# Two sums of the down weights moved to VectorE, and an embedding gate by plain products

## The chip, the cores and the metric

The kernel runs on one core of a Trainium2 chip. Its time is the device time of one execution in microseconds (us); given are the median and the extremes of several. A profile is taken of one further execution. The engines are TensorE (PE, matrix products into PSUM banks), VectorE (DVE), ScalarE (ACT), GpSimd (POOL) and SyncE (SP); the last two, and ScalarE now and then, issue DMAs.

## The reference

One layer of a decoder trunk in fp32 for 512 tokens, width 1024, feed-forward width 2816. The change touches its two last parts:

```python
for i in range(DEPTH):                     # DEPTH = 1
    ...
    h = rmsnorm(x, ffn_norm[i])
    x = x + conv_ffn(h, w_up[i], conv_w[i], conv_b[i], w_down[i])
    gate = jax.nn.sigmoid((rmsnorm(x, ple_norm[i]) @ w_ple_gate[i]).astype(jnp.float32)).astype(x.dtype)
    x = x + gate * (p[i] @ w_ple[i])
return rmsnorm(x, final_norm)
```

`conv_ffn` is a product with w_up (1024 x 5632), a causal convolution of width 3, gelu(a) * b, and a product with w_down (2816 x 1024).

## The kernel before

**Products.** Every fp32 product is three fp32r matmuls of split operands (`mm3`, L203 to L207): high by high, high by low, low by high. Weights come as raw blocks of 128x1024 and are split by `parts` (L64): a cast on ScalarE gives the high part (L69), a subtraction on VectorE the low part (L70). The parts go to four rotating buffers, or, with `spare`, to the pool of 37 blocks (`blk`) that also holds raw blocks and operands.

**Queue of weights.** `plan`, `plan_seven`, `prepare` and `take` (L89 to L160) form one list of units, in the order in which the products use them. A unit is a load (DMA) and a cut (sums and split). Four loads are issued ahead of the cut that is due, and two cuts are made ahead of the product that takes them. So loads stand on SyncE's queue, and casts and subtractions on ScalarE's and VectorE's, in program order among everything else that these engines do.

**Seven products for eight.** `seven` (L349) computes a product of 2x2 blocks with seven block products P1 to P7 of combined operands. The weights are quartered into a, b, c, d. Combined weights: P1 takes a, P5 a+b, P6 a+b+c, P7 b+c, P4 a+b+c+d, P2 d, P3 c. P6, P7 and P4 accumulate into two PSUM banks (`seeded`, sd) that start as copies of P1. Behind P6, and again behind P7, ScalarE copies these banks out (`u`, L372); the next product that adds to them waits for the copies. `minus` (L374) subtracts on VectorE, and a drain takes each finished quarter.

**Down product.** The loop over the 22 blocks of the feed-forward width makes the combined operands; after eight, sixteen and 22 blocks the down product runs for 4, 4 and 3 pairs of blocks (`PARTS`, L37) by `seven` in the order P1 P5 P2 P6 P7 P4 P3 (`DOWN`): rounds one, two and three below. Its weights are planned with `adds="all"` (L198): a block t starts as b, GpSimd DMAs that accumulate add a (for P5), then c (for P6, issued after P5's split, L141), then d (for P4, after P6's split); a block s starts as b, and a GpSimd DMA adds c (for P7). Each for two chunks (two contraction tiles each) of a round: eight accumulating DMAs a round. The drain adds the result to x (L682).

**Gate.** After round three x's columns are turned by TensorE transposes (`turn_half`, L720), scaled on ScalarE, combined on VectorE and split. Between the two halves of the tokens stands the embedding product p @ w_ple for the first two token tiles (`embed`, L648; the other two were made earlier, put into the DRAM tile `ple_d`, and are read back at L745). The gate's product is `seven` in the order P5 P1 P6 P7 P4 P2 P3 (`LAST`) with the quartered w_g planned with `adds="some"` (L201): a and c (for s) by GpSimd DMAs, c for P6 and d for P4 by sums on VectorE (L138). `tail` halves the last quarter. `drain_g` (L765) applies sigmoid, multiplies by the embedding, adds to x, squares, and for a finished token tile makes the reciprocal root on GpSimd (`rstd_1`, L608), scales by it and the final norm's weights `gB`, and writes out.

Of the kernel before, what the change touches and what calls it, by code (L numbers as in the profile page):

```python
# [7 lines left out]
F32 = mybir.dt.float32  # L8
# [26 lines left out]
DOWN = ("P1", "P5", "P2", "P6", "P7", "P4", "P3")  # L35
LAST = ("P5", "P1", "P6", "P7", "P4", "P2", "P3")
PARTS = ((0, 4), (4, 4), (8, 3))  # L37
# [8 lines left out]
def trunk(ctx, tc, xT, xr, pT, wsT, par, bsp, w_u0, w_u1, w_v, w_ga, w_gb, w_p, w_pl,  # L46
# [46 lines left out]
    def plan_seven(w, order=INNER, adds="vector", spare=(), q0=0, n=HK):  # L93
# [25 lines left out]
        def unit(prod, ch):  # L119
            inplace = adds == "vector"  # L120
            t = "a" if inplace else "t"
            need = {"P1": [("a", "a")], "P5": [("b", "b")] if inplace else [("t", "b", "a")],
                    "P6": [] if adds == "all" else [("c", "c")], "P7": [] if inplace else [("s", "b", "c")],
                    "P4": [] if adds == "all" else [("d", "d")], "P2": [("d", "d")], "P3": [("c", "c")]}[prod]
            dst = {"P1": "a", "P5": t, "P6": t, "P7": "b" if inplace else "s", "P4": t, "P2": "d", "P3": "c"}[prod]
            extra = {"P5": "b" if inplace else None, "P6": "c", "P7": "c" if inplace else None, "P4": "d"}.get(prod)
            if adds == "all":
                extra = None
            cols = ch[1] * T

# [12 lines left out]

            todo.append((load, cut))

        for prod in order:
            for ch in pairs_of(n):
                unit(prod, ch)

# [22 lines left out]
    for w in (w_v, w_ga, w_gb):  # L172
        plan_seven(blocks(w))

# [16 lines left out]
    for i in range(KF):  # L191
# [156 lines left out]

    def seven(op, drain, order=INNER, fill=(), tail=False):  # L349

        fill = list(fill)
        n = len(op)
        ahead = AHEAD + 2 if tail else AHEAD
        bank_of = {}
# [3 lines left out]
        def step(o, c, w, ch, first):  # L360
            for j, c0, m, t in o:
                for i in range(ch[1]):
                    k = ch[0] + i
                    a = op[k][c]
                    a = [a[:, z, j * P:(j + 1) * P] for z in range(2)]
                    mm3(t, a, [z[:, c0:c0 + m] for z in wslice(w, i, T)], first and k == 0, k == n - 1,
                        skip_group_check=True)

# [4 lines left out]

        def minus(p, z):  # L374
            j, c0, m, t = p
            o = z[j][:, c0:c0 + m]
            V.tensor_tensor(o, t, o, op=ALU.subtract)
            return o

        for prod in order:  # L380
            b, c = ops[prod]
            if b not in bank_of:
                bank_of[b] = [(j, 0, T, seeded[j] if b == "b" else bank()) for j in range(2 if b != "c" or not tail else 1)]
                if b == "c" and tail:
                    bank_of[b] += [(1, 0, H, bank()[:, :H]), (1, H, H, bank()[:, :H])]
            o = bank_of[b]
            first = b != "b" and b not in begun
            begun.add(b)
            if prod == "P3" and tail:
                ws = [take(ahead) for _ in pairs_of(n)]  # L390
                for p in o:
                    for w, ch in zip(ws, pairs_of(n)):
                        step([p], c, w, ch, False)
                    drain(0, p[0], 1, minus(p, u[0]), p[1])
                continue
            for ch in pairs_of(n):
                step(o, c, take(ahead), ch, first)
                if fill:
                    fill.pop(0)()
            if prod == "P1":  # L400
                for j in range(2):
                    S.copy(seeded[j], o[j][3])
            elif prod == "P6":
                copies(0)
            elif prod == "P7":
                copies(1)
                for p in bank_of["c"]:
                    minus(p, u[1])
                for j in range(2):
                    drain(1, j, 1, u[1][j], 0)  # L410
            elif prod == "P4":
                for j in range(2):
                    drain(1, j, 0, seeded[j], 0)
            elif prod == "P2":
                for p in o:
                    drain(0, p[0], 0, p[3], 0)
            elif prod == "P3":
                for p in o:
                    drain(0, p[0], 1, minus(p, u[0]), 0)
        for f in fill:  # L420
# [67 lines left out]

    def drain_v(th, j, fh, src, c0):
        b = 2 * th + j  # L490
# [33 lines left out]
    def gate(op, fill=()):  # L524
        g = [None] * NT

        def drain(th, j, fh, src, c0):
            b = 2 * th + j
# [150 lines left out]
    def drain_x(last):  # L679
        def drain(th, j, fh, src, c0):  # L680
            b = 2 * th + j
# [37 lines left out]

    def turn_half(th, k):  # L720
        tp = bank()
        for i, f in enumerate((k, HK + k)):
            for j in range(2):
                PE.transpose(tp[:, (2 * i + j) * P:(2 * i + j + 1) * P], columns(x, 2 * th + j, f), ident)
        t = block("xf", (4, H))
        for i, f in enumerate((k, HK + k)):
            S.activation(t[:, i], tp[:, i * H:(i + 1) * H], AF.Copy, scale=col(C_PLE, f))  # L727
        return t

    G1 = []  # L730
    for k in range(HK):
        t = turn_half(1, k)
        V.tensor_tensor(t[:, 2], t[:, 0], t[:, 1], op=ALU.subtract)
        z = halves(t[:, 1:3], 2)
        G1.append((t, z))
    ple = [block("ple") for _ in range(NT)]
# [10 lines left out]
    for k in range(HK):  # L747
# [5 lines left out]
        if k % 2 == 0:  # L753
            t2 = block("s2", (2, 2, H), F32R)
        cut_into(t2[:, k % 2], t1[:, 3])
        z0, z3 = halves(t[:, 0:2], 2), halves(t[:, 2:4], 2)
        XE.append(dict(A11=z0[:, 0], A12=z0[:, 1], A22=z1[:, 0], D=z1[:, 1], S2=t2[:, k % 2], S3=z3[:, 0], E=z3[:, 1]))
    r_emb = [rstd_1([xss[b][:, 0:1], xss[b][:, 1:2]]) for b in range(NT)]


    fss = [small.tile([P, 3], F32, tag="fss", name="fss", bufs=NT) for _ in range(NT)]
    seen = [0] * NT
    done = [0] * NT

    def drain_g(th, j, fh, src, c0):  # L765
        b = 2 * th + j
        n = src.shape[-1]
        last = b == 1
        pc = ple[b][:, fh, c0:c0 + n]
        xc = x[b][:, fh, c0:c0 + n]  # L770
        S.activation(src, src, AF.Sigmoid, scale=r_emb[b])
        V.tensor_tensor(pc, src, pc, op=ALU.mult)
        V.tensor_tensor(xc, xc, pc, op=ALU.add)  # L773
        S.activation(src, xc, AF.Square, accum_out=fss[b][:, seen[b]:seen[b] + 1])
        if last:
            V.tensor_tensor(pc, xc, gB[:, fh * T + c0:fh * T + c0 + n], op=ALU.mult)
        seen[b] += 1
        done[b] += n
        if done[b] == D:
            r = rstd_1([fss[b][:, i:i + 1] for i in range(seen[b])])  # L780
            for g in range(2):
                ot = ple[b][:, g]
                if not last:
                    V.scalar_tensor_tensor(ot, x[b][:, g], r, gB[:, g * T:(g + 1) * T], op0=ALU.mult, op1=ALU.mult)  # L784
                elif g:
                    S.activation(ot, ot, AF.Copy, scale=r)
                else:
                    V.tensor_scalar_mul(ot, ot, r)
                nc.sync.dma_start(out[b, :, g * T:(g + 1) * T], ot)

    seven(XE, drain_g, LAST, tail=True)


# [4 lines left out]
def _layout(i):  # L798
# [22 lines left out]
    def pairs(z):  # L821
# [25 lines left out]
        "w_dn": a["w_down"][0].reshape(KF // 2, 2, P, 2, T).transpose(1, 3, 0, 2, 4).reshape(4, KF // 2, P, T),  # L847
        "w_g": sv(a["w_ple_gate"][0]),
        "w_ple": a["w_ple"][0].reshape(2, P, D),
# [17 lines left out]
```

## Time and profile before

| | |
|---|---|
| median of 3 runs | 807.81 us (807.12 to 807.92) |
| profiled execution, its own time | 809.77 us |
| its span in the trace | 808.1 us |
| its mean granted TensorE clock | 0.986 |
| TensorE busy | 773.3 us (96%) |
| VectorE busy | 553.9 us (69%) |
| ScalarE busy | 389.6 us (48%) |
| GpSimd busy | 60.5 us (7%) |

Times in the rows are microseconds from the start of the span. Busy shares are means over stages with different limits; matmuls overlap in the pipeline, so one lasts longer (0.39 us) than the distance to the next. "idle before <-releaser" is the time for which the engine had nothing to do, and what ended it. A granted clock of 1.00 is 2.4 GHz.

### The profile page before, as it was taken

To read this page: it belongs to the slowest core of one execution; us is meant where nothing else is said; L and a number is where in the kernel's file an instruction comes from. 1 tells how busy PE (TensorE), PEld (TensorE's weight loads), DVE (VectorE), ACT (ScalarE), POOL (GpSimd) and SP (SyncE) were. 2 spreads that over 40 slices of the span, in tenths; PEclk is the share of its full clock that TensorE was granted. 3 is DMA by queue.
4 is the path that set the end of the run, shared out by engine and by line. 5 is a ranking of instruction groups with operands and counts; after the bars stand their busy time and mean duration, and the time that the engine had idled before them with its cause. 6 is when DMAs were issued, how large, how long until landed. Compare 5 with 4: busy or idle time off the path is not lost.

```text
span 808.1 us, 9316 instructions
## 1 busy us (share of the span) xinstructions
PE 773.3 (96%) x3458; PEld 635.6 (79%) x3458; DVE 553.9 (69%) x783; ACT 389.6 (48%) x566; POOL 60.5 (7%) x95
## 2 busy tenths in 40 slices
PE   9999999999999999999999997999999799999793
PEld 7888888888888887888888875888888588877673
DVE  7796988774666646336766663676774566778896
ACT  6676745562232324225644543345443434467873
POOL 0000100000122000000000021000013010031101
PEclk9999999999999999999999998999999899999997
DMA  9612225152044256006422369631229862391712
GB/s 350 253 53 79 78 79 183 53 191 96 1 156 150 85 173 218 1 1 268 174 53 66 91 133 269 216 93 46 78 79 212 244 168 78 107 194 26 239 22 104
DMA packets 42493, 104.26 MB, mean 129 GB/s; under 512 B 3664, under 2 KB 3792, under 8 KB 42448
## 3 DMA queue, kind: packets, MB, share of 16 engines
q1 hardware_dynamic: 33760, 85.73, 30.3%
q0 software_dynamic: 7104, 13.63, 10.0%
q10 hardware_dynamic: 1584, 4.31, 1.6%
q8 instruction: 27, 0.44, 0.2%
q14 instruction: 18, 0.15, 0.1%
HBM read 100.51 MB, written 3.15 MB: 128 GB/s over the span
## 4 chain that ended last, share of the span: by engine, by line
PE 47%; issue 27%; DMA 11%; DVE 8%; ACT 5%; POOL 1%; POOLq 0%; SPq 0%; ACTq 0%; DVEq 0%
PE mm L205 10%; PE mm L206 10%; PE mm L207 10%; DMA raw<-in_w_dn 9%; PE sd L205 6%; PE sd L206 6%; PE sd L207 6%; DVE wlo L70 2%; ACT whi L69 2%; DMA pt<-in_pT 1%; DVE raw L138 1%; POOL raw L106 1%; PE mm L514 1%; DVE x L773 0%; DVE ple L784 0%
## 5 line engine op out<-in xcount | busy, mean ns | idle before, releaser
L70 DVE TENSOR_TENSOR wlo<-raw,whi 128x1024 fp32r<-128x1024 f32 (+1 forms) x192 | 225.3, 1182 | 184.2 <-ACT whi L69 183.6
L69 ACT CAST whi<-raw 128x1024 fp32r<-128x1024 f32 (+1 forms) x185 | 189.8, 1032 | 232.4 <-PE mm L206 56.2
L206 PE MATMUL mm<-blk,whi 128*128 128x512 f32 x480 | 186.8, 389 | 0.0
L205 PE MATMUL mm<-blk,whi 128*128 128x512 f32 x480 | 186.4, 390 | 0.3 <-ACT blk L240 0.3
L207 PE MATMUL mm<-blk,wlo 128*128 128x512 f32 x480 | 186.6, 389 | 0.0
L205 PEld LDWEIGHTS mm<-blk,whi 128*128 128x128 f32 x480 | 90.0, 188 | 19.6 <-ACT blk L240 0.9
L206 PEld LDWEIGHTS mm<-blk,whi 128*128 128x128 f32 x480 | 90.1, 188 | 18.8
L207 PEld LDWEIGHTS mm<-blk,wlo 128*128 128x128 f32 x480 | 90.1, 188 | 18.6
L205 PE MATMUL mm<-whi,blk 128*128 128x512 f32 x214 | 83.9, 392 | 1.2 <-ACT xf L727 1.2
L206 PE MATMUL mm<-wlo,blk 128*128 128x512 f32 x214 | 83.4, 390 | 0.0
L207 PE MATMUL mm<-whi,blk 128*128 128x512 f32 x214 | 83.3, 389 | 0.0
L205 PE MATMUL sd<-whi,cmb 128*128 128x512 f32 x108 | 45.5, 421 | 12.8 <-ACT u L372 12.3
L205 PE MATMUL mm<-whi,cmb 128*128 128x512 f32 (+1 forms) x132 | 50.1, 380 | 2.1 <-ACT xf L727 1.8
L106 POOL DMA_DIRECT2D raw<-in_w_dn x24 | 27.9, 1389 | 321.9 <-DVE wlo L70 207.6
L206 PE MATMUL mm<-wlo,cmb 128*128 128x512 f32 (+1 forms) x132 | 49.8, 377 | 0.4 <-DVE wlo L70 0.4
L207 PE MATMUL mm<-whi,cmb 128*128 128x512 f32 (+1 forms) x132 | 49.3, 376 | 0.0
L205 PEld LDWEIGHTS mm<-whi,blk 128*128 128x128 f32 x214 | 40.2, 188 | 10.3 <-ACT xf L727 2.0
L207 PEld LDWEIGHTS mm<-whi,blk 128*128 128x128 f32 x214 | 40.2, 188 | 8.3
L206 PEld LDWEIGHTS mm<-wlo,blk 128*128 128x128 f32 x214 | 40.2, 188 | 8.2
L206 PE MATMUL sd<-wlo,cmb 128*128 128x512 f32 x108 | 44.3, 410 | 0.3 <-DVE wlo L70 0.3
L207 PE MATMUL sd<-whi,cmb 128*128 128x512 f32 x108 | 43.9, 408 | 0.0
L205 PE MATMUL sd<-whi,blk 128*128 128x512 f32 x110 | 43.1, 392 | 0.5 <-ACT u L372 0.5
(184 smaller groups left out, 1037.2 us busy)
## 6 DMA issues: line engine op xcount, KB each, us to landing
raw<-in_w_up SPq DMA_DIRECT2D x44, 512.0 KB, 5.5
raw<-in_w_dn SPq DMA_DIRECT2D x25, 512.0 KB, 3.4
raw<-in_w_dn POOLq DMA_DIRECT2D x20, 512.0 KB, 7.8
raw<-in_w_g SPq DMA_DIRECT2D x10, 512.0 KB, 6.7
raw<-in_w_v SPq DMA_DIRECT2D x8, 512.0 KB, 11.4
raw<-in_w_ga SPq DMA_DIRECT2D x8, 512.0 KB, 4.0
raw<-in_w_gb SPq DMA_DIRECT2D x8, 512.0 KB, 3.6
raw<-in_w_p SPq DMA_DIRECT2D x8, 512.0 KB, 4.8
```

The lines of the kernel that those rows point to most:

```text
L69: (V.tensor_copy if first else S.copy)(hi[:, :cols], raw[:, :cols])
L70: V.tensor_tensor(lo[:, :cols], raw[:, :cols], hi[:, :cols].bitcast(F32), op=ALU.subtract)
L106: (G if kw else nc.sync).dma_start(o, block_of(name, ch), **kw)
L138: V.tensor_tensor(z[:, :cols], z[:, :cols], raw[extra, ch][:, :cols], op=ALU.add)
L205: PE.matmul(o, wh, ah, start=first, stop=False, **kw)
L206: PE.matmul(o, wh, al, start=False, stop=False, **kw)
L207: PE.matmul(o, wl, ah, start=False, stop=last, **kw)
L514: PE.matmul(mx[:, n * P:(n + 1) * P], vt[n].rearrange("p a t -> p (a t)")[:, f * P:(f + 1) * P], wsm[:, f, :], start=True, stop=True)
```

## The change

**Down weights.** `plan_seven` is called with `"some"` instead of `"all"`: c (for P6) and d (for P4) are loaded to blocks of their own and added by VectorE in the unit's cut. a for P5 and c for P7 still come by accumulating GpSimd DMAs. c's block is loaded for P6 and kept for P3, so that the number of plain loads stays ten a round. VectorE gets four sums a round (rounds one and two: of 128x1024; round three: two of 128x1024 and two of 128x512), GpSimd loses four DMAs.

**Gate.** w_g is eight plain blocks (128 rows by 1024 columns), all split once into blocks that are kept. The operands are only turned and split. Token tiles run in the order 2, 3, 0, 1; each has eight contraction steps for two banks (the last tile: one bank of 512 columns, then two of 256). The second half's columns are turned ahead of token tile 3. The multiplication by gB now stands ahead of the reciprocal root for all tiles. `tail`, `LAST` and the column argument of the drains are gone.

```diff
-            plan_seven(blocks(w_dn), DOWN, "all", q0=part[0], n=part[1])
+            todo.extend(plan_seven(blocks(w_dn), DOWN, "some", q0=part[0], n=part[1]))
     for k in range(2):
         plan(w_ple[k])
-    plan_seven(blocks(w_g), LAST, "some", spare=("P3",))
+    for k in range(KD):
+        plan(w_g[k], spare=True)
...
-    def turn_half(th, k):
...
+    def turn_half(th):
+        got = []
+        for k in range(HK):
+            tp = bank()
+            t = block("xe", (2, 2, H), F32R)
+            for i, f in enumerate((k, HK + k)):
+                for j in range(2):
+                    PE.transpose(tp[:, (2 * i + j) * P:(2 * i + j + 1) * P], columns(x, 2 * th + j, f), ident)
+            for i, f in enumerate((k, HK + k)):
+                split_into(t[:, i], tp[:, i * H:(i + 1) * H], col(C_PLE, f))
+            got.append(t)
+        return got
+
+    XE = [None, turn_half(1)]
...
-    XE = []
-    for k in range(HK):
-        t1, z1 = G1[k]
-        t = turn_half(0, k)
-        V.tensor_tensor(t1[:, 3], t1[:, 2], t[:, 0], op=ALU.subtract)
-        V.tensor_tensor(t[:, 2], t[:, 0], t1[:, 0], op=ALU.subtract)
-        V.tensor_tensor(t[:, 3], t[:, 1], t1[:, 3], op=ALU.add)
...
+    wg = [take() for _ in range(KD)]
...
-    seven(XE, drain_g, LAST, tail=True)
+    for b in (2, 3, 0, 1):
+        th, j = divmod(b, 2)
         last = b == 1
...
+        if b == 3:
+            XE[0] = turn_half(0)
+
         if last:
+            groups = [[(bank(), 0)], [(bank()[:, :H], T)], [(bank()[:, :H], T + H)]]
+        else:
+            groups = [[(bank(), 0), (bank(), T)]]
+        fss = small.tile([P, 3], F32, tag="fss", name="fss")
+        n = 0
+        for group in groups:
+            for k in range(KD):
+                a = XE[th][k % HK][:, k // HK]
+                a = [a[:, z, j * P:(j + 1) * P] for z in range(2)]
+                for ob, c0 in group:
+                    mm3(ob, a, [z[:, c0:c0 + ob.shape[-1]] for z in wg[k]], k == 0, k == KD - 1)
+            for ob, c0 in group:
...
+                S.activation(ob, ob, AF.Sigmoid, scale=r_emb[b])
+                V.tensor_tensor(pc, ob, pc, op=ALU.mult)
+                V.tensor_tensor(xc, xc, pc, op=ALU.add)
+                S.activation(ob, xc, AF.Square, accum_out=fss[:, n:n + 1])
+                V.tensor_tensor(pc, xc, gB[:, c0:c0 + w], op=ALU.mult)
+                n += 1
```

Below stand the orders of single engines, of the program before and of the changed one. Line numbers are those of the program that the rows come from; they are smaller in the changed one.

GpSimd's queue in round one of the down product, before. raw_3629 and raw_3686 are the blocks t of the two chunks, raw_3819 and raw_3838 the blocks s; what stands in brackets are the semaphores of the instructions waited for (DVE: VectorE, DMAHW: plain loads, DMASW: GpSimd's own DMAs).

```order
L106 DMA raw_3629<-in_w_dn 128x2x512 [waits DMAHW5_49,DMAHW2_49,DMAHW6_49,DMAHW0_49,DVE_49]
L106 DMA raw_3629<-in_w_dn 128x2x512 [waits DMASW0_49,DVE_49]
L106 DMA raw_3686<-in_w_dn 128x2x512 [waits DMAHW5_49,DMAHW3_49,PE_49]
L106 DMA raw_3686<-in_w_dn 128x2x512 [waits DMASW2_49,DVE_49]
L106 DMA raw_3819<-in_w_dn 128x2x512 [waits DMAHW4_49,DMAHW6_49,DMAHW0_49,PE_49]
L106 DMA raw_3838<-in_w_dn 128x2x512 [waits DMAHW7_49]
L106 DMA raw_3629<-in_w_dn 128x2x512 [waits DMASW1_49,DVE_49]
L106 DMA raw_3686<-in_w_dn 128x2x512 [waits DMASW3_49,DVE_49]
```

The same queue in the changed program: round one's four (raw_3629 and raw_3686 are t, raw_3821 and raw_3840 are s), and the first of round two.

```order
L105 DMA raw_3629<-in_w_dn 128x2x512 [waits DMAHW5_49,DMAHW2_49,DMAHW6_49,DMAHW0_49,DVE_49]
L105 DMA raw_3686<-in_w_dn 128x2x512 [waits DMAHW5_49,DMAHW3_49,DVE_49]
L105 DMA raw_3821<-in_w_dn 128x2x512 [waits DMAHW5_49,DMAHW4_49,DMAHW7_49,DMAHW0_49,DVE_49]
L105 DMA raw_3840<-in_w_dn 128x2x512 [waits DMAHW5_49,DMAHW7_49,DMAHW1_49,DVE_49]
L105 DMA raw_4553<-in_w_dn 128x2x512 [waits DMAHW4_49,DMAHW0_49,DVE_49]
```

The second and third writes into t are gone, and the two DMAs into s stand directly behind the first writes. The waits for VectorE that are left are for buffers that come free, no longer for splits of this round.

VectorE in round three, before, from the splits for P6 on. raw_5241 (128x1024) and raw_5286 (128x512) are t of the two chunks; x_2521 and x_2522 are the sums that drain P2; raw_5425 and raw_5438 are s, for P7.

```order
L70 TENSOR_TENSOR wlo_5442<-raw_5241,whi_5441 128x1024
L70 TENSOR_TENSOR wlo_5459<-raw_5286,whi_5458 128x512
L682 TENSOR_TENSOR x_2521<-mm_5373,x_2521 128x512
L682 TENSOR_TENSOR x_2522<-mm_5374,x_2522 128x512
L611 TENSOR_SCALAR fms_5810<-xss_3034 128x1
L611 TENSOR_SCALAR fms_5815<-xss_3035 128x1
L70 TENSOR_TENSOR wlo_5476<-raw_5425,whi_5475 128x1024
L70 TENSOR_TENSOR wlo_5494<-raw_5438,whi_5493 128x512
```

VectorE at the same place in the changed program; raw_5393 and raw_5409 are c, raw_5318 and raw_5375 are d, raw_5427 is s.

```order
L137 TENSOR_TENSOR raw_5241<-raw_5241,raw_5393 128x1024
L137 TENSOR_TENSOR raw_5286<-raw_5286,raw_5409 128x512
L666 TENSOR_TENSOR x_2521<-mm_5373,x_2521 128x512
L69 TENSOR_TENSOR wlo_5445<-raw_5241,whi_5444 128x1024
L69 TENSOR_TENSOR wlo_5462<-raw_5286,whi_5461 128x512
L666 TENSOR_TENSOR x_2522<-mm_5374,x_2522 128x512
L137 TENSOR_TENSOR raw_5241<-raw_5241,raw_5318 128x1024
L137 TENSOR_TENSOR raw_5286<-raw_5286,raw_5375 128x512
L595 TENSOR_SCALAR fms_5722<-xss_3034 128x1
L595 TENSOR_SCALAR fms_5727<-xss_3035 128x1
L69 TENSOR_TENSOR wlo_5478<-raw_5427,whi_5477 128x1024
```

The sums for P6 stand ahead of P2's drain and the splits for P6 between its two halves; the sums for P4 come ahead of the split for P7.

SyncE's queue at the gate, before, from the embedding's weights on.

```order
L82 DMA raw<-in_w_ple 128x1024 x2
L106 DMA raw<-in_w_g 128x2x512 x5
L745 DMA ple<-ple_d 128x512 x4
L106 DMA raw<-in_w_g 128x2x512 x5
L789 DMA out<-ple 128x512 x8
```

The same queue in the changed program.

```order
L81 DMA raw<-in_w_ple 128x1024 x2
L81 DMA raw<-in_w_g 128x1024 x6
L727 DMA ple<-ple_d 128x512 x4
L81 DMA raw<-in_w_g 128x1024 x2
L768 DMA out<-ple 128x512 x8
```

Six blocks of w_g instead of five quarters' chunks stand ahead of the reads of ple_d, two instead of five behind them.

## Rows read from the trace of the kernel before

**Rows 1.** The page: busy time with share of span; granted clock in 40 slices.

```profile
PE 773.3 (96%) x3458; PEld 635.6 (79%) x3458; DVE 553.9 (69%) x783; ACT 389.6 (48%) x566; POOL 60.5 (7%) x95
...
PEclk9999999999999999999999998999999899999997
```

**Rows 2.** Table by stretches: undisturbed, rounds one, two, three, gate to end.

```profile
core 0: us, PE busy (x) PEld busy (x) DVE busy (x) ACT busy (x) POOL busy (x), PEclk, DMA share, GB/s
550.00:600.00 50.00, 50.00 (x222) 41.43 (x221) 34.81 (x49) 22.65 (x31) 0.00 (x0) 1.00 0.20 64
472.73:519.56 46.83, 41.40 (x169) 33.32 (x168) 24.65 (x27) 18.74 (x23) 6.03 (x5) 0.93 0.88 236
606.60:652.87 46.27, 40.87 (x169) 33.27 (x168) 24.60 (x27) 18.73 (x23) 7.07 (x6) 0.93 0.89 232
707.27:738.31 31.04, 29.48 (x128) 23.37 (x127) 22.92 (x34) 20.59 (x36) 7.59 (x7) 1.00 0.73 142
738.31:808.10 69.79, 50.82 (x249) 40.10 (x247) 57.86 (x108) 46.62 (x88) 7.28 (x10) 0.94 0.34 106
```

**Rows 3.** Sum of waits of TensorE: total us, times, longest us.

```profile
PE sd L205 <- ACT u L372: 12.8, 5, 5.4
```

**Rows 4.** Timeline of TensorE: start, us, instruction, idle before and its releaser.

```profile
500.39 0.79 PE L205 MATMUL sd<-whi,cmb 128*128 128x512 f32 x1 [5.07 <-ACT u L372]
...
506.37 0.39 PE L207 MATMUL sd<-whi,cmb 128*128 128x512 f32 x1
...
633.92 0.80 PE L205 MATMUL sd<-whi,cmb 128*128 128x512 f32 x1 [5.40 <-ACT u L372]
...
726.73 0.50 PE L205 MATMUL sd<-whi,cmb 128*128 128x512 f32 x1 [1.07 <-ACT u L372]
```

**Rows 5.** Timeline of ScalarE in round one.

```profile
489.54 1.05 ACT L69 CAST whi<-raw 128x1024 fp32r<-128x1024 f32 x1 [5.08 <-DMA raw<-in_w_dn]
...
498.81 1.04 ACT L69 CAST whi<-raw 128x1024 fp32r<-128x1024 f32 x1 [1.50 <-DMA raw<-in_w_dn]
499.76 1.07 ACT L372 COPY u<-sd 128x512 f32<-128x512 f32 x2
```

**Rows 6.** Timeline of GpSimd in round one: all its DMA issues.

```profile
469.95 2.42 POOL L106 DMA_DIRECT2D raw<-in_w_dn  x2 [59.92 <-DVE wlo L70]
481.88 3.65 POOL L106 DMA_DIRECT2D raw<-in_w_dn  x3 [9.51 <-DVE wlo L70]
486.21 1.19 POOL L106 DMA_DIRECT2D raw<-in_w_dn  x1 [0.69 <-DVE wlo L70]
492.15 1.20 POOL L106 DMA_DIRECT2D raw<-in_w_dn  x1 [4.75 <-DVE wlo L70]
```

**Rows 7.** Line L106 on GpSimd, whole span: from issue to landing.

```profile
DMA to landing us min/median/max: 4.4/7.8/13.4
```

**Rows 8.** Groups by line and form on VectorE, 560 to 809: busy, mean ns.

```profile
L138 DVE TENSOR_TENSOR raw<-raw 128x1024 f32<-128x1024 f32 x4 | 4.8, 1224 | 0.0
```

**Rows 9.** Timeline of VectorE in round three.

```profile
719.03 1.37 DVE L682 TENSOR_TENSOR x<-mm,x 128x512 f32<-128x512 f32 x2 [1.43 <-PE mm L207]
...
722.13 1.82 DVE L70 TENSOR_TENSOR wlo<-raw,whi 128x1024 fp32r<-128x1024 f32 x2 [0.79 <-ACT whi L69]
```

**Rows 10.** Timeline of SyncE at the gate.

```profile
751.15 2.75 SPq L745 DMA_DIRECT2D ple<-ple_d  x4
753.98 3.56 SPq L106 DMA_DIRECT2D raw<-in_w_g  x5
```

**Rows 11.** Line L106 on SyncE, 745 to 780: from issue to landing.

```profile
DMA to landing us min/median/max: 6.1/7.7/8.1
```

**Rows 12.** Timelines of TensorE and of ScalarE at the end.

```profile
795.45 0.28 PE L206 MATMUL mm<-wlo,cmb 128*128 128x256 f32 x1
795.57 0.28 PE L207 MATMUL mm<-whi,cmb 128*128 128x256 f32 x1
...
801.62 0.42 ACT L774 ACTIVATE u<-x 128x256 f32<-128x256 f32 x1 [2.47 <-DVE x L773]
```

More of the change, by code (lines that the diff above doesn't have):

```diff
@@ L142, in cut @@
                 return o
[L144 to L148, printed above, removed]
+            return load, cut
+        return [unit(prod, ch) for prod in order for ch in pairs_of(n)]
     def prepare(loads=LOADS):
@@ L172, in trunk @@
     for w in (w_v, w_ga, w_gb):
-        plan_seven(blocks(w))
+        todo.extend(plan_seven(blocks(w)))
     def plan_map(g2):
@@ L347, in trunk, with seven @@
            "P2": ("a", "A12"), "P3": ("c", "E")}
-    def seven(op, drain, order=INNER, fill=(), tail=False):
+    def seven(op, drain, order=INNER, fill=()):
         fill = list(fill)
         n = len(op)
-        ahead = AHEAD + 2 if tail else AHEAD
         bank_of = {}
@@ L365, in step @@
                     a = [a[:, z, j * P:(j + 1) * P] for z in range(2)]
-                    mm3(t, a, [z[:, c0:c0 + m] for z in wslice(w, i, T)], first and k == 0, k == n - 1,
-                        skip_group_check=True)
+                    mm3(o[j], a, wslice(w, i, T), first and k == 0, k == n - 1, skip_group_check=True)
         def copies(i):
@@ L372, in copies, with minus @@
                 S.copy(u[i][j], seeded[j])
[L374 to L378, printed above, removed]
+        def minus(i):
+            for j in range(2):
+                V.tensor_tensor(u[i][j], bank_of["c"][j], u[i][j], op=ALU.subtract)
         for prod in order:
@@ L382, in seven @@
             if b not in bank_of:
-                bank_of[b] = [(j, 0, T, seeded[j] if b == "b" else bank()) for j in range(2 if b != "c" or not tail else 1)]
-                if b == "c" and tail:
-                    bank_of[b] += [(1, 0, H, bank()[:, :H]), (1, H, H, bank()[:, :H])]
+                bank_of[b] = seeded if b == "b" else [bank() for _ in range(2)]
             o = bank_of[b]
@@ L388, in seven @@
             begun.add(b)
[L389 to L395, printed above, removed]
             for ch in pairs_of(n):
-                step(o, c, take(ahead), ch, first)
+                step(o, c, take(), ch, first)
                 if fill:
@@ L406, in seven @@
                 copies(1)
-                for p in bank_of["c"]:
-                    minus(p, u[1])
+                minus(1)
                 for j in range(2):
-                    drain(1, j, 1, u[1][j], 0)
+                    drain(1, j, 1, u[1][j])
             elif prod == "P4":
                 for j in range(2):
-                    drain(1, j, 0, seeded[j], 0)
+                    drain(1, j, 0, seeded[j])
             elif prod == "P2":
-                for p in o:
-                    drain(0, p[0], 0, p[3], 0)
+                for j in range(2):
+                    drain(0, j, 0, o[j])
             elif prod == "P3":
-                for p in o:
-                    drain(0, p[0], 1, minus(p, u[0]), 0)
+                minus(0)
+                for j in range(2):
+                    drain(0, j, 1, u[0][j])
         for f in fill:
@@ L525, in gate, with drain @@
         g = [None] * NT
-        def drain(th, j, fh, src, c0):
+        def drain(th, j, fh, src):
             b = 2 * th + j
@@ L717, in trunk @@
             seven(hc[q0:q0 + n], drain_x(q0 + n == KF // 2), DOWN)
-    def turn_half(th, k):
[L721 to L730, printed above, removed]
-    for k in range(HK):
[L732 to L735, printed above, removed]
+    def turn_half(th):
[4 more added lines that the diff above has]
+            for i, f in enumerate((k, HK + k)):
+                for j in range(2):
+                    PE.transpose(tp[:, (2 * i + j) * P:(2 * i + j + 1) * P], columns(x, 2 * th + j, f), ident)
[4 more added lines that the diff above has]
+    XE = [None, turn_half(1)]
     ple = [block("ple") for _ in range(NT)]
```

54 lines of the change are left out of this document (16 added, 38 removed).

## The prediction

> **What bounds the kernel now.** I read the page first. TensorE is busy 773.3 of 808.1 us, and its granted clock is below full in two places near the last third of the span [rows 1]. A table by stretches puts these in the down product's rounds one and two [rows 2]. An undisturbed stretch of 50 us holds 222 matmuls of 512 columns at clock 1.00, 0.2267 us each [rows 2]; a round of eight contraction tiles (parts one and two) issues 7 products x 4 x 2 token tiles x 3 = 168 of them, 38.1 us. Round one takes 46.83 us and round two 46.27, both at clock 0.93; round three, with 126 matmuls (28.6 us), takes 31.04 [rows 2]. So the losses are 8.7, 8.2 and 2.5 us.
>
> The sum of waits names the place: TensorE waits 12.8 us for the copies of the seeded banks, in five waits [rows 3]. The two large ones are 5.07 and 5.40 us, and behind the first, 14 matmuls take from 500.39 to 506.37, 0.427 us each and so about half rate (1.2 GHz instead of 2.4), where 14 at full rate take 3.2: 2.8 us more, and the second stall looks the same [rows 4]. ScalarE made the copies late although TensorE had finished their product at 495.3 (500.39 less 5.07) [rows 4]: ahead of them in its order stand casts of down weights, each waiting for a DMA, the first 5.08 us, the last starting at 498.81 [rows 5]. The DMAs are GpSimd's accumulating ones. Its queue is in order: an issue for P6 waits until 481.88 for a split on VectorE, two sums for P7 that depend on no split leave right behind it, and P4's leave at 486.21 and 492.15 [rows 6]. They land 4.4 to 13.4 us after their issue, 7.8 in the middle [rows 7]. So the cast of 489.54 (P6's second chunk) starts 7.7 us after the issue of 481.88, and the cast of 498.81 (P4's first) 12.6 after that of 486.21.
>
> From 738.31, where the gate's transposes start, to the end are 69.8 us, of which VectorE is busy 57.9 [rows 2]. TensorE's last matmul starts at 795.57, so the last 12 us are drains, with ScalarE once waiting 2.47 us for VectorE [rows 12].
>
> **The change, part by part.** *Sums of P6 and P4, rounds one and two.* Four of eight accumulating DMAs per round go; four VectorE sums come. Their nearest row is the sum of 128x1024 in the gate, 1224 ns [rows 8]: 4.9 us a round. VectorE is busy 24.65 of the 46.83 us [rows 2], so about 29.5 of 38.1 would be used, and all four sums stand ahead of the x sums that wait for P2's end. Their inputs are plain loads, one of them (block c) now issued for P6 rather than for P3; the number of loads is unchanged. On GpSimd four DMAs a round remain, none of which waits for a split: P7's two can leave with the round's first, by about 473 at 1.2 each instead of behind 481.88 [rows 6], and the slowest landing of 13.4 [rows 7] gives 486, while TensorE comes to P7 some 24 us after 470. The casts then no longer wait, the copies come straight behind P6, and both stalls and the half rate behind them go. What is late next: VectorE's share of P6 and P4 (two sums and two splits, 4.9 us, against 5.4 us of TensorE for a product). It starts ahead, since in the old order it idled waiting for these casts. I take nothing left: 8.7 + 8.2 = 16.9 us gained. Bounds: 16.9, and about 13 if VectorE ends up to 2 us late in each round.
>
> *Round three.* Its stalls are short: the largest 1.07 us [rows 4]. There the new order puts the x sum of P2's first half ahead of P6's first split. That sum cannot start before TensorE ends that half (719.03 before, behind an idle of 1.43) and takes half of that row's 1.37 [rows 9]; the split behind it takes about 1.2 [rows 8], so it is ready near 720.9, while TensorE comes to P6 at about 719.5 and needs the split with its second matmul. That is a new stall of some 0.9, and I leave another 0.9 of the old ones: gain 0.7, bounds 0 and 2.4.
>
> *Gate.* The product has 144 + 24 matmuls of 512 columns and 48 of 256, instead of 156 and 24. At 0.2267 and 0.12 us [rows 2, 12] that is 43.8 instead of 38.2 us, 5.6 more. What goes: all VectorE and ScalarE work on combined operands, four sums and four accumulating DMAs of weights, six of the fourteen weight splits. Before, TensorE's work from 738.31 (product 38.2, embedding 24 x 0.2267 = 5.4, 32 transposes at about 0.1) was 47 of 69.8 us, so 10.5 us were idle inside and 12.3 behind it. Now, with t counted from 738.31: the first half's eight operand splits and the embedding fill 9.1 us; weight blocks 0 to 5 are split one after the other at VectorE's pace (1.15 to 1.22 each), and the first token tile uses six matmuls, 1.36 us, for each, so that it has used block 5 at t = 17.0. Blocks 6 and 7 are loaded behind the reads of ple_d in SyncE's queue. Those reads wait for VectorE's small copies and left at 751.15, and the five w_g loads behind them at 753.98 [rows 10]; in the new order the copies end near 10.9, the reads take 2.7 to issue, and the two loads leave at 13.6 and 14.2. Loads of this kind landed after 6.1 to 8.1 us [rows 11]; with fewer beside them I take 5 to 6 (my bound of 8.1 is the row's): 18.6 and 19.4, split by 20.8 and 21.95. TensorE idles 2.6 us ahead of block 6 and 0.9 ahead of its second matmul. The first tile ends at 23.1; with the second half's transposes the other tiles take 10.9 each, the last in pieces: matmuls end at 57.2. VectorE has 5.2 us of drain for each 10.9 us, so no backlog. The last quarter's sigmoid, product and sum, 0.4 to 0.5 each with hand-overs, take 2.2 to the last square, and from the last square to the end are 6.5 us (801.62 to 808.1) [rows 12]. End: 57.2 + 2.2 + 6.5 = 65.9, against 69.8: **gain 3.9**. Bounds: with no wait for blocks 6 and 7, 63.9 (gain 5.9); with landings of 8.1 us and the half rate behind the longer idle, 69.3 + 2.8 = 72.1 (loss 2.3).
>
> On that idle the rows say: after 1.07 us the clock stayed at full rate (round three is at 1.00), after 5.07 it fell to half [rows 2, 4]; 2.6 us lies between them, nearer to the first, so I charge no half rate. The Trainium skill, "TensorE: Matmul & The Clock Gate", section "HAM oscillation — how this bites in real kernels", speaks against this part: a contraction loop whose work per weight tile is shorter than the wait for the next tile's DMA is sent back to the slow clock after each wait. By that rule, the first token tile would be slowed behind block 6, and perhaps behind block 7; the trace shows such a fall only behind 5 us stalls. The rival "gate gives back" below is this mechanism, priced from rows.
>
> **Rivals.** *Gate gives back.* Blocks 6 and 7 land as late as the slowest row, TensorE idles 5 us or more and runs at half rate after it: the gate loses 2.3 at most instead of winning 3.9, so 792.5. For it: the reads stand ahead of the loads, and landings of 6.1 to 8.1 [rows 10, 11]. Against: those five shared the engines with the reads and each other.
>
> *VectorE on the path.* Sums ahead of splits make P6 and P4 late by 1 to 2 us a round, as I expect in round three: 786.3 + 3 = 789 to 790. For: two sums and two splits are 4.9 of 5.4 us. Against: the idle ahead of them [rows 5].
>
> *More than forecast.* Round three's loss disappears (+1.7) and blocks 6 and 7 come in time (+2): 782.6.
>
> *Slower: P7's DMAs are the real limit.* If the accumulating DMAs of block c land late for another reason than the queue ahead of them (their own landing, or the loads beside them), P7's casts stay late, the copies wait behind them as before, and both stalls remain, while the gate pays its 5.6 us of additional matmuls with no idle to fill: 807.8 + 5.6 = 813.4. It decides if they land later than P7's turn, over 20 us after they leave; the longest landing is 13.4 [rows 7]. If the edit to the sums does nothing and the gate wins its 3.9, the time would be 804.
>
> **How the numbers follow.** Sum: 8.7 + 8.2 + 0.7 + 3.9 = 21.5. The profiled execution took 809.77 us (its span 808.1): 788.3. The median of the runs shown is 807.81, 1.96 lower, and I take the difference off that: **786.3**. Chances: forecast 0.62, gate gives back 0.17, VectorE on the path 0.10, more than forecast 0.08, slower 0.03. The range 782 to 795 takes in the gate's whole span of bounds and VectorE's on top of it. About 0.2% (1.6 us) is what a measurement of this kernel can tell from no change. All but the last case, and a rest of 0.02 in which half of the gain fails and the gate loses much, are faster: faster 0.95, same 0.02, slower 0.03.
>
> **What would show it.** Rounds one and two about 38 us each at clock 1.00 in the table by stretches; no wait over 1 us of TensorE for the copies there; ScalarE's casts without DMA waits; four GpSimd issues a round, close together. In round three a VectorE split right behind the x sum, with TensorE waiting for it. In the gate, a TensorE wait of 2 to 4 us for the cast of a w_g block in the first token tile, no VectorE backlog at the end, and some 66 us from the first transpose to the end. The prediction is wrong if casts still wait for P7's DMAs, if the clock falls again in the first gate tile, or if TensorE waits for splits of P6 or P4 in rounds one and two.

## The result and the profile after

The changed kernel takes 786.6 us (785.42 to 787.91, four executions) beside 807.87 (807.12 to 809.1) of the kernel before: ratio 0.9736, 95% interval 0.9714 to 0.9758, 21.3 us less. The forecast was 786.3, with a range of 782 to 795. The profiled execution is the slowest of the four, 787.91 us, with a span of 786.2, 21.9 less than the span before.

The table by stretches of the changed kernel shows where they went (start and end, length, busy us of each engine with its instructions, granted clock, DMA share, GB/s). Rounds one, two, three, and the gate from its first transpose to the end; the last row is six microseconds inside the gate:

```profile
472.04:510.12 38.08, 38.08 (x169) 31.53 (x168) 29.10 (x31) 19.04 (x23) 0.00 (x0) 1.00 0.64 207
597.16:635.24 38.08, 38.08 (x169) 31.53 (x168) 29.10 (x31) 19.04 (x23) 0.86 (x2) 1.00 0.64 200
689.64:720.20 30.56, 29.51 (x127) 23.36 (x126) 26.03 (x38) 19.45 (x35) 0.00 (x0) 1.00 0.16 52
720.20:786.20 66.00, 55.51 (x273) 46.05 (x271) 39.04 (x82) 30.68 (x61) 5.99 (x8) 0.94 0.20 72
...
739.00:745.00 6.00, 4.25 (x11) 3.16 (x11) 4.41 (x7) 3.95 (x7) 0.00 (x0) 0.72 0.01 3
```

Against [rows 2]: round one 46.83 to 38.08 (8.75 less), round two 46.27 to 38.08 (8.19), round three 31.04 to 30.56 (0.48), gate 69.79 to 66.00 (3.79). Round one also starts 0.69 earlier. The change touches nothing that TensorE does ahead of it, and over the runs below that start lies anywhere from 471.47 to 474.84, so the 0.69 is taken as scatter. Together 21.9. In rounds one and two TensorE is busy all the time at clock 1.00.

The sum of TensorE's waits (total us, times, longest), where 12.8 us for the copies stood in [rows 3]:

```profile
PE mm L203 <- DVE xe L239: 1.4, 1, 1.4
PE mm L203 <- ACT whi L68: 1.2, 1, 1.2
...
PE sd L203 <- ACT u L367: 1.1, 2, 0.8
PE sd L204 <- DVE wlo L69: 0.8, 1, 0.8
PE mm L204 <- DVE wlo L69: 0.8, 1, 0.8
```

GpSimd's and ScalarE's timelines in round one, to be read against [rows 6] and [rows 5]:

```profile
429.45 1.20 POOL L105 DMA_DIRECT2D raw<-in_w_dn  x1 [19.94 <-issue]
462.29 1.19 POOL L105 DMA_DIRECT2D raw<-in_w_dn  x1 [31.64 <-DMA raw<-in_w_dn]
470.02 1.20 POOL L105 DMA_DIRECT2D raw<-in_w_dn  x1 [6.54 <-DVE cmb L331]
...
491.33 1.05 ACT L68 CAST whi<-raw 128x1024 fp32r<-128x1024 f32 x1 [1.66 <-PE sd L205]
492.64 0.59 ACT L367 COPY u<-sd 128x512 f32<-128x512 f32 x1 [0.26 <-PE sd L205]
494.00 0.59 ACT L367 COPY u<-sd 128x512 f32<-128x512 f32 x1 [0.77 <-PE sd L205]
```

P7's two sums leave at 462.29 and 470.02 instead of behind 481.88. The round's four issues are not close together, as the prediction had it, but spread from 408.13 on; none waits for a split. The casts no longer wait for a DMA: most wait for TensorE, which frees the buffers of the parts, and the one at 481.70 waits 2.48 us for VectorE's sum for P6, early enough for TensorE. P4's first cast still stands ahead of the copies (at 491.33), but now each copy follows directly the half of P6 that it copies.

The gate, at the last two blocks of w_g (6 and 7, counted from 0): SyncE, ScalarE and TensorE of the profiled execution.

```profile
729.96 2.52 SPq L727 DMA_DIRECT2D ple<-ple_d  x4
732.57 0.86 SPq L81 DMA_DIRECT2D raw<-in_w_g  x2
...
738.89 1.04 ACT L68 CAST whi<-raw 128x1024 fp32r<-128x1024 f32 x1 [5.24 <-DMA raw<-in_w_g]
...
739.99 0.50 PE L203 MATMUL mm<-whi,xe 128*128 128x512 f32 x1 [1.23 <-ACT whi L68]
741.25 0.74 PE L204 MATMUL mm<-wlo,xe 128*128 128x512 f32 x1 [0.76 <-DVE wlo L69]
...
744.76 0.40 PE L203 MATMUL mm<-whi,xe 128*128 128x512 f32 x1
```

The two loads stand behind the reads, TensorE waits 1.23 and 0.76 us, and the eight matmuls from 741.25 to 744.76 take 3.51 us where eight at full rate take 1.81: the clock fell to half there (granted 0.72 over the six microseconds in the table).

### The profile page after: what moved, and what is told of

Read it like the earlier page. It is cut to its first block, busy times and chain, and to the rows that moved or that the text cites. A ratio compares the mean times of both kernels' runs of the same rounds, so it can differ in the third digit from the quotient of the medians.

```text
span 786.2 us, 9275 instructions
## 1 busy us (share of the span) xinstructions
PE 771.4 (98%) x3482; PEld 637.8 (81%) x3482; DVE 547.2 (70%) x769; ACT 372.9 (47%) x538; POOL 42.8 (5%) x79
## 4 chain that ended last, share of the span: by engine, by line
PE 89%; DVE 4%; DMA 2%; ACT 2%; issue 1%; POOL 0%; POOLq 0%; SPq 0%; ACTq 0%; DVEq 0%
PE mm L203 24%; PE mm L204 23%; PE mm L205 23%; PE sd L204 6%; PE sd L203 6%; PE sd L205 6%; DVE wlo L69 1%; ACT whi L68 1%; DMA pt<-in_pT 1%; DMA raw<-in_w_g 1%; PE mm L498 1%; DVE raw L137 1%; PE mm L614 0%; DMA x<-in_xT 0%; DVE xn L649 0%
## 5 line engine op out<-in xcount | busy, mean ns | idle before, releaser
L69 DVE TENSOR_TENSOR wlo<-raw,whi 128x1024 fp32r<-128x1024 f32 (+1 forms) x186 | 217.9, 1179 | 158.2 <-ACT whi L68 157.8
L68 ACT CAST whi<-raw 128x1024 fp32r<-128x1024 f32 (+1 forms) x179 | 183.7, 1031 | 214.7 <-PE mm L204 56.8
L203 PE MATMUL sd<-whi,blk 128*128 128x512 f32 x110 | 43.1, 392 | 0.3 <-ACT u L367 0.3
L204 PE MATMUL sd<-wlo,blk 128*128 128x512 f32 x110 | 42.8, 389 | 0.0
L205 PE MATMUL sd<-whi,blk 128*128 128x512 f32 x110 | 42.8, 389 | 0.0
L137 DVE TENSOR_TENSOR raw<-raw 128x1024 f32<-128x1024 f32 (+1 forms) x36 | 42.0, 1199 | 0.1
L203 PE MATMUL sd<-whi,cmb 128*128 128x512 f32 x92 | 36.2, 395 | 0.8 <-ACT u L367 0.8
L204 PE MATMUL sd<-wlo,cmb 128*128 128x512 f32 x92 | 36.1, 392 | 0.8 <-DVE wlo L69 0.8
L205 PE MATMUL sd<-whi,cmb 128*128 128x512 f32 x92 | 35.8, 389 | 0.0
L205 PE MATMUL mm<-whi,cmb 128*128 128x512 f32 x92 | 35.8, 389 | 0.0
```

The source lines that it names most:

```text
L68: (V.tensor_copy if first else S.copy)(hi[:, :cols], raw[:, :cols])
L69: V.tensor_tensor(lo[:, :cols], raw[:, :cols], hi[:, :cols].bitcast(F32), op=ALU.subtract)
L203: PE.matmul(o, wh, ah, start=first, stop=False, **kw)
L204: PE.matmul(o, wh, al, start=False, stop=False, **kw)
L205: PE.matmul(o, wl, ah, start=False, stop=last, **kw)
```

## Experiments

Ratios are to the kernel before, run on the same chip beside each, with their 95% intervals in brackets.

**Each half alone.** The edit to the down weights in the old kernel, and the new gate with the old sums:

```diff
-            plan_seven(blocks(w_dn), DOWN, "all", q0=part[0], n=part[1])
+            plan_seven(blocks(w_dn), DOWN, "some", q0=part[0], n=part[1])
```

> The kernel before with the edit to the down weights alone (P6's and P4's sums on VectorE in all three rounds; the gate as before). My account: the rounds' losses go here and nowhere else, so rounds one and two take 38.1 us each, round three 30.6, the gate from its first transpose to the end stays at 69.8: 807.9 less 8.7, 8.2 and 0.5 is 790.5. Rival: part of it is given back in the old gate, whose VectorE is busy 58 of 70 us and whose weight loads now start elsewhere: 792 or more, and the gate over 71 us.

791.73 us (791.27 to 793.93), ratio 0.9805 (0.9788 to 0.9821). Its rounds and its gate:

```profile
474.84:512.92 38.08, 38.08 (x169) 31.53 (x168) 29.11 (x31) 19.03 (x23) 0.00 (x0) 1.00 0.68 209
599.96:638.04 38.08, 38.08 (x169) 31.53 (x168) 29.10 (x31) 19.03 (x23) 0.89 (x1) 1.00 0.68 203
692.44:723.00 30.56, 29.51 (x127) 23.36 (x126) 26.04 (x38) 20.52 (x36) 0.00 (x0) 1.00 0.21 52
723.00:792.20 69.20, 50.77 (x249) 40.08 (x247) 57.83 (x108) 46.62 (x88) 7.30 (x10) 0.95 0.35 107
```

The rounds are those of the changed kernel to the hundredth, and the old gate gives nothing back (69.20 against 69.79). The median lies between the 790.5 of the account and the 792 of the rival, whose longer gate did not come. The profiled execution is the slowest of the four; its round one starts 2.1 us later than before, in a part that both kernels share.

```diff
-            todo.extend(plan_seven(blocks(w_dn), DOWN, "some", q0=part[0], n=part[1]))
+            todo.extend(plan_seven(blocks(w_dn), DOWN, "all", q0=part[0], n=part[1]))
```

> The changed kernel with the down weights summed by GpSimd as before: only the gate is changed. My account: rounds 46.8, 46.3 and 31.0 us with the two 5 us waits for the copies, the gate 66.0 us with a fall of the clock behind block 6, 64 without: 804.1 or 802. Rival: the 3.8 us seen in the gate come from GpSimd's and the DMA engines' lighter load out of round three and are lost here: 807 to 809.

801.78 us (800.65 to 803.76), ratio 0.9934 (0.9914 to 0.9953). Rounds and gate:

```profile
471.47:517.29 45.82, 41.30 (x169) 33.55 (x168) 24.75 (x27) 18.73 (x23) 6.04 (x5) 0.93 0.90 240
604.33:650.87 46.54, 40.87 (x170) 33.23 (x169) 24.61 (x27) 18.74 (x23) 7.07 (x6) 0.93 0.87 231
705.27:734.95 29.68, 29.19 (x127) 23.45 (x126) 22.91 (x34) 19.42 (x35) 5.15 (x5) 1.00 0.60 130
734.95:798.90 63.95, 54.19 (x273) 44.80 (x271) 39.05 (x82) 30.69 (x61) 5.99 (x8) 0.96 0.20 75
```

The gate's gain is its own. Here the cast of block 6 came earlier (TensorE waited 0.36 and 0.76 us), the matmuls behind it stayed at full rate, and the gate took 63.95 instead of 66.00. The two halves' savings, 15.8 and 5.7 us by the medians, add up to the whole, 21.3. Round three, with the old sums, took 29.68, less than with VectorE's.

**Which of the two sums.** Only P4's, then only P6's, on VectorE (in all rounds):

```diff
-            if adds == "all":
+            if adds == "all" or (adds == "d" and prod == "P6") or (adds == "c" and prod == "P4"):
                 extra = None
...
-                if adds == "all" and prod in ("P5", "P6"):
-                    add_to(z, "c" if prod == "P5" else "d", ch)
+                if prod == "P5" and adds in ("all", "d"):
+                    add_to(z, "c", ch)
+                if prod == "P6" and adds in ("all", "c"):
+                    add_to(z, "d", ch)
...
-            plan_seven(blocks(w_dn), DOWN, "all", q0=part[0], n=part[1])
+            plan_seven(blocks(w_dn), DOWN, "d", q0=part[0], n=part[1])
```

The second run passes `"c"` in the last line.

> The kernel before with only P4's sum (block d) moved to VectorE; P6's (block c) stays an accumulating GpSimd DMA that waits for P5's split, and P7's two stand behind it in the queue. My account, by the queue: P7's second sum still leaves near 484, its cast comes at 493 to 496 and the copies behind it, so TensorE still waits 1 to 3.5 us in rounds one and two, with or without half rate behind: 795 to 803. Rival, only the cast that stands directly ahead of the copies (P4's first chunk) matters: no wait over 1 us, 790.5.

797.65 us (797.36 to 797.88), ratio 0.988 (0.9865 to 0.9895). Round one's queue and copies, and TensorE's waits for the copies in rounds one and two:

```profile
481.02 3.65 POOL L106 DMA_DIRECT2D raw<-in_w_dn  x3 [8.76 <-DVE wlo L70]
...
493.59 1.99 ACT L69 CAST whi<-raw 128x1024 fp32r<-128x1024 f32 x2 [2.86 <-DMA raw<-in_w_dn]
495.49 1.06 ACT L374 COPY u<-sd 128x512 f32<-128x512 f32 x2
...
496.12 0.50 PE L207 MATMUL sd<-whi,cmb 128*128 128x512 f32 x1 [1.57 <-ACT u L374]
...
625.15 0.80 PE L207 MATMUL sd<-whi,cmb 128*128 128x512 f32 x1 [2.58 <-ACT u L374]
```

> The kernel before with only P6's sum (block c) moved to VectorE; P4's (block d) stays an accumulating GpSimd DMA that waits for P6's split. My account: P7's first sum leaves early, P4's first one after P6's split near 484 to 485 and lands 8 to 12 us later, its cast is at 493 to 497 and the copies right behind it: TensorE waits 0 to 2.5 us per round, 790.5 to 799. Rival, P6's sum alone was the cause: no wait, 790.5. Rival, P4's alone: the waits stay near 5 us, 805 to 808.

799.41 us (798.39 to 802.59), ratio 0.9908 (0.9886 to 0.9931):

```profile
484.01 3.65 POOL L106 DMA_DIRECT2D raw<-in_w_dn  x3 [20.99 <-DVE wlo L70]
...
492.81 1.99 ACT L69 CAST whi<-raw 128x1024 fp32r<-128x1024 f32 x2 [6.17 <-DMA raw<-in_w_dn]
494.71 1.07 ACT L374 COPY u<-sd 128x512 f32<-128x512 f32 x2
...
495.34 0.50 PE L207 MATMUL sd<-whi,cmb 128*128 128x512 f32 x1 [1.67 <-ACT u L374]
...
624.32 0.80 PE L207 MATMUL sd<-whi,cmb 128*128 128x512 f32 x1 [3.57 <-ACT u L374]
```

That is a little above the 790.5 to 799 expected, and the second wait above the 0 to 2.5 us. Either sum left on GpSimd keeps a wait of 1.6 to 3.6 us: what it waits for (a split) holds up what is queued behind it, and its own or P7's cast stands ahead of the copies. Neither sum alone was the cause. In both kernels the clock stayed up behind the wait of round one, 1.57 and 1.67 us (the first matmul takes 0.50, the next 0.39 or 0.40), and fell behind that of round two, 2.58 and 3.57 (0.80, then 0.63).

**The order on ScalarE.** All sums as before, but each of P4's casts first gets one column from a copied bank, so that the copies stand ahead of it:

```diff
+    mark = []
+
...
+        if mark:
+            S.copy(hi[:, :1], mark.pop()[:, :1])
         (V.tensor_copy if first else S.copy)(hi[:, :cols], raw[:, :cols])
...
                 S.copy(u[i][j], seeded[j])
+            if order is DOWN and i == 0:
+                mark.extend(2 * [u[i][1]])
```

> The kernel before, all sums as they were, but ScalarE's casts for P4 are made to stand behind its copies of the seeded banks (a one-column copy from a copied bank into each cast's target first). Tests whether the order on ScalarE, not the lateness of P4's weights, stops TensorE. My account: the copies then follow P7's casts near 497, TensorE waits about 2.5 us instead of 5 in rounds one and two, with or without half rate behind: 797 to 803. Rival: P4's and P7's late weights stop TensorE themselves, so that the wait only changes its name: 806 or more.

802.09 us (801.66 to 802.76), ratio 0.9931 (0.9915 to 0.9946):

```profile
494.93 1.05 ACT L73 CAST whi<-raw 128x1024 fp32r<-128x1024 f32 x1 [1.54 <-DMA raw<-in_w_dn]
495.88 1.07 ACT L376 COPY u<-sd 128x512 f32<-128x512 f32 x2
...
496.51 0.50 PE L209 MATMUL sd<-whi,cmb 128*128 128x512 f32 x1 [2.48 <-ACT u L376]
...
497.24 0.63 PE L211 MATMUL sd<-whi,cmb 128*128 128x512 f32 x1
...
627.37 0.80 PE L209 MATMUL sd<-whi,cmb 128*128 128x512 f32 x1 [3.19 <-ACT u L376]
```

With no DMA moved, the waits for the copies fell from 5.07 and 5.40 to 2.48 and 3.19 us. Waits of TensorE for P4's weights did not come in their place. About half of the old wait was the place of P4's cast on ScalarE, not a lack of weights on TensorE; the rest stands behind P7's casts, whose sums are still late. The clock fell behind both waits, behind the shorter one with its second or third matmul (0.63).

**The queue at the gate.** The changed kernel again, and with the reads of ple_d on ScalarE's queue, so that the eight w_g loads stand in a row:

```diff
-            nc.sync.dma_start(ple[2 + b][:, fh], ple_d[b, fh])
+            nc.scalar.dma_start(ple[2 + b][:, fh], ple_d[b, fh])
```

> The changed kernel once more, beside the two variants of its gate. Executions in which the clock falls behind block 6 should take about 2 us more than those in which it does not: 784 to 788, mean clock 0.999 for the short ones.

> The changed kernel with the four reads of ple_d issued from ScalarE's queue, so that all eight w_g loads stand in a row on SyncE's. My account: blocks 6 and 7 are split in time, TensorE no longer waits in the first token tile, the clock stays at full rate there: gate 62 to 64 us, total 782 to 784.5. Rival: blocks 6 and 7 wait for buffers or for VectorE's splits, not for the queue: the wait stays and the total is that of the changed kernel.

The changed kernel again: 785.12 us (784.31 to 787.91), ratio 0.9726 (0.9706 to 0.9746). With the reads moved: 784.22 (784.09 to 784.75), ratio 0.971 (0.9695 to 0.9724). A repetition of the latter stands beside the runs on round three:

> The changed kernel with the reads of ple_d on ScalarE's queue, once more, as the base for the two runs beside it: 784.2, round three 30.5 us, gate 62.8 us.

784.91 us (784.12 to 786.3), ratio 0.9721 (0.9702 to 0.974). The gate in the second profile of the changed kernel:

```profile
720.65:783.40 62.75, 53.89 (x273) 44.80 (x271) 39.05 (x82) 30.70 (x61) 5.98 (x8) 0.98 0.21 76
```

And with the reads moved, in the first of the two:

```profile
719.66:782.50 62.84, 53.63 (x273) 44.91 (x271) 38.87 (x82) 30.48 (x61) 5.98 (x8) 0.98 0.18 68
```

From issue to landing, the two late loads in the first profile of the changed kernel, whose gate took 66.00:

```profile
DMA to landing us min/median/max: 6.3/6.7/7.0
```

The same in its second profile:

```profile
DMA to landing us min/median/max: 4.2/4.6/5.0
```

So two microseconds of landing cost 3.25 us of gate where the clock falls, and nothing is left to win where they land early. Executions of 787 to 788 us are three of eight of the changed kernel and none of nine with the reads moved; on the medians the intervals overlap, so that it is a smaller scatter rather than a proven gain. That every long execution is one in which the clock fell in the gate is not shown: the two of 787.91 have the lowest mean clock (0.995), but 787.38 and the shortest, 784.31, both have 0.997, where 0.999 was expected for the short ones.

**The embedding first.** As the last, with the embedding of token tiles 0 and 1 ahead of the first transposes:

```diff
-    XE = [None, turn_half(1)]
     ple = [block("ple") for _ in range(NT)]
...
     c_ple = [take(), take()]
     for b in range(2):
         for fh in range(2):
             embed(b, fh, ple[b][:, fh])
+    XE = [None, turn_half(1)]
```

> As the run with the reads on ScalarE's queue, and the embedding product for token tiles 0 and 1 moved ahead of the first transposes, so that it covers round three's last drain and the splits of the first operands. My account: the 1.4 us wait in the embedding and the waits for the first operands go, 0.5 to 2 us less than that run: 781 to 783.5. Rival: the embedding's banks and copies stand in the way of the transposes and of their splits, and the first tile starts as late as before: no gain over that run.

786.42 us (785.36 to 788.98), ratio 0.974 (0.9719 to 0.9762): no gain, as the rival said, but for another reason than it gave. The wait in the embedding went; the reads now stand behind the operand splits on ScalarE and ahead of the casts of w_g, and TensorE waits there:

```profile
729.94 2.55 ACTq L729 DMA_DIRECT2D ple<-ple_d  x4
732.53 5.80 ACT L68 CAST whi<-raw 128x1024 fp32r<-128x1024 f32 x6 [2.55 <-issue]
...
733.62 0.73 PE L203 MATMUL mm<-whi,xe 128*128 128x512 f32 x2 [2.03 <-ACT whi L68]
```

**Round three.** On the base with the reads moved, P6's sum, then both sums, of round three back on GpSimd (the first run's call; the second has `"all"` for `"d"`, and `plan_seven` knows `"d"` as above):

```diff
-            todo.extend(plan_seven(blocks(w_dn), DOWN, "some", q0=part[0], n=part[1]))
+            todo.extend(plan_seven(blocks(w_dn), DOWN, "some" if part[1] == 4 else "d", q0=part[0], n=part[1]))
```

> That base, with round three's sum for P6 back on GpSimd's queue (only P4's on VectorE); rounds one and two stay as changed. VectorE then has P6's splits ahead of the sum that drains P2. My account: the 0.8 us wait for P6's split (with the restart about 1.2) is the price of that order in round three, so round three takes 29.3 to 29.6 instead of 30.5, total 783 to 783.4. Rival: the GpSimd sum is as late as before and another wait takes the place: round three 30.5 or more.

> That base, with both of round three's sums on GpSimd's queue, as in the kernel before. Round three took 31.04 and 29.68 us in two executions with this order. My account: 29.5 to 31 by the landing of P4's sum, total 783.2 to 784.7, with more scatter than the run with one sum on VectorE. Rival: VectorE's sums are needed in round three too: 31 or more, total 784.7 or more.

783.98 us (783.13 to 784.73), ratio 0.9707 (0.969 to 0.9725), and 783.48 (783.28 to 785.1), ratio 0.9702 (0.9685 to 0.9719). Round three of the base:

```profile
690.09:720.68 30.59, 29.54 (x128) 23.37 (x127) 26.05 (x38) 19.50 (x35) 0.00 (x0) 1.00 0.20 69
```

With P6's sum on GpSimd:

```profile
690.58:720.05 29.47, 29.21 (x128) 23.45 (x126) 24.39 (x36) 19.63 (x35) 3.03 (x3) 1.00 0.49 123
```

With both:

```profile
690.87:720.52 29.65, 29.16 (x127) 23.44 (x126) 22.91 (x34) 19.43 (x35) 5.15 (x5) 1.00 0.67 148
```

About 1 us less in the round in both. The totals go the same way, with intervals that overlap that of the base; the first is a little above the 783 to 783.4 expected.

## Why the prediction was right, and where not

**Rounds one and two: right, and for the reason given.** Forecast 38.1 us each at clock 1.00, measured 38.08. P7's DMAs wait for no split; the casts wait for no DMA; VectorE's sums cost nothing visible (29.10 of 38.08 us busy, forecast 29.5). For the order on ScalarE the run with the copies first is the proof: it moves no DMA and takes away about half of the wait. For the order on GpSimd the runs with one sum speak. With P6's sum on VectorE, one of P7's DMAs left at 461.84, and the cast of its block (at 485.59, by the order of the casts) waited for no DMA; the other stood behind P4's first, which left at 484.01, and the next casts waited 6.17 us for DMAs. These runs also issue two GpSimd DMAs fewer a round, and no run changes the order of that queue alone, so what the lighter traffic gave is not separated. One point of the working was incomplete. It read the casts ahead of the copies as an effect of late DMAs; the run with the copies first shows that about half of the wait lay in the place of P4's cast alone. Written behind the copies in the program, it was put ahead of them by the scheduler that orders each engine, and the account of the kernel ahead of the prediction, which says that casts stand in program order, is wrong in this point.

**Round three: mechanism right, sign wrong.** The wait behind the sum that drains P2 was forecast at 0.9 and is 0.79, with the splits behind the first half of that drain as said:

```profile
701.40 0.69 DVE L666 TENSOR_TENSOR x<-mm,x 128x512 f32<-128x512 f32 x1 [1.43 <-PE mm L205]
702.01 1.82 DVE L69 TENSOR_TENSOR wlo<-raw,whi 128x1024 fp32r<-128x1024 f32 x2
```

In [rows 9] both halves of the drain come ahead of the splits. Of the 0.7 us of gain 0.48 came, by the two profiles. But the term took 31.04 us as what GpSimd's sums cost in this round, and that was one execution's value: the new gate with the old sums took 29.68, and the run with both sums back on GpSimd 29.65. Against these the change loses about 1 us in round three. The medians agree: the edit to the down weights alone saved 15.8 us, 1.1 less than rounds one and two gained by the profiles.

**The gate: the sum right by luck, since several of its terms were wrong and cancelled.** 65.9 us forecast, 66.00 measured, with t counted from the first transpose. The two loads left at t = 12.4 and 12.8 (13.6 and 14.2 by the working) and landed after 6.3 to 7.0 us (5 to 6 assumed), so that block 6's first matmul came at t = 19.8 (19.65 by the working). TensorE's idle ahead of it was 1.23 and not 2.6 because twelve of the second half's sixteen transposes, written ahead of the second tile, ran within the first, and block 5 was done at 18.6 instead of 17.0. The half rate, for which nothing was charged, did come, and cost 1.7 us; that the clock falls again in the first gate tile is one of the signs by which the prediction said it would be wrong, and in this part it was. The last matmul therefore ended at about t = 58.9 instead of 57.2, and the tail gave that back: 7.1 us from there to the end, against 8.7 taken from [rows 12] with their backlog. Where the loads landed early, the gate took 62.75, 3 us less than forecast.

That is also the place of the rule that spoke against the change, in the Trainium skill, "TensorE: Matmul & The Clock Gate", section "HAM oscillation — how this bites in real kernels": where the work on a weight tile is shorter than the wait for the next tile's DMA, TensorE is back at the slow clock when the next tile starts. The trace comes near it in the execution with 66.00 us, where a block is 1.36 us of work and eight matmuls at 0.44 us each follow waits of 1.23 and 0.76, which are longer than that only together; it does not show it in those where the loads landed in time (waits of 0.28, or 0.36 and 0.76). The prediction took the length of the single idle as its measure; a wait of 1.39 us in the embedding of the same profile left the clock up, while two shorter ones with one matmul between them did not.

**The total: within 0.3 us, and partly luck.** Round three lost about 1 us where 0.7 of gain was forecast, and the gate gained more than forecast in the executions with early loads; the two errors go against each other.

**The rivals.** "Gate gives back" was right in its mechanism, a wait with the half rate behind it, and too large in its price: a wait of 1.23 us and 1.7 us of half rate, not 5 us and a loss of the whole gain. "VectorE on the path" held in round three only. "More than forecast" came by half: in the profiled execution of 785.18 us the gate took 62.75, but round three kept its loss. The slower case fell: of all twelve accumulating DMAs that are left, P7's among them, none landed later than 8.1 us after its issue:

```profile
DMA to landing us min/median/max: 4.6/6.0/8.1
```

## What to carry to other kernels

Where the busiest engine waits for a small copy, look at what stands ahead of the copy on its own engine, and follow that to the head of the queue that it waits for: here one DMA that waits for a split held up two that do not, a cast that waits for a DMA stood ahead of the copies, and at the end TensorE stood still for 5 us and ran at half rate for 6. A stall term should be taken from more than one execution where it hangs on when DMAs land: round three's 31.04 us were 29.7 in others. When a weight block is to arrive in the middle of a contraction loop, put its load ahead of every DMA in its queue that waits for something; here that made the times scatter less.

## What was not expected of the hardware

The same two loads of 512 KB, issued at the same place of the same program, landed after 4.2 to 5.0 us in one execution and 6.3 to 7.0 in another. In the second TensorE waited longer and the clock fell, and the gate took 3.25 us more, 0.4% of the kernel.

Behind a single wait the clock stayed at full rate after 1.39 us (embedding), 1.57, 1.67 and 1.82 (down product) and 2.03 (gate, embedding first), and fell after 2.48, 2.58, 3.19 and 3.57; behind 1.23 and 0.76 us with one matmul between them it fell too. The lengths of the waits alone do not decide it. In the old gate, waits of 0.90 to 0.92 and of 1.28 us, with four transposes between them, left the clock up in the kernel before and in three of the runs with that gate; in the fourth, with the copies first, it fell behind 0.91 and 1.28 (granted 0.50 from 743 to 746 us). The twelve transposes behind the second wait, before and in that run:

```profile
750.22 1.63 PE L724 MATMUL mm<-ident,x 128*128 128x128 f32 x12 [1.28 <-ACT ple L652]
```

```profile
742.42 2.67 PE L730 MATMUL mm<-ident,x 128*128 128x128 f32 x12 [1.28 <-ACT ple L658]
```

What tells the two apart no run shows.
